# The odd layer's five engine queues, ordered by a planner in the kernel instead of by the framework's scheduler

## The chip, the cores and the metric

The kernel runs on one core of a Trainium2 chip. The metric is the device time of one launch in microseconds (us), less being better. The core has five instruction queues that run side by side, each strictly in order: TensorE (PE, matmuls), VectorE (DVE), ScalarE (ACT), GpSimd (POOL), and SyncE (SP), which here issues the DMA transfers. An instruction at the head of its queue that waits for another engine or a transfer holds up all that stand behind it in that queue.

## The reference

A trunk of two layers over 1024 tokens of width 1024, all float32, and a final RMSNorm. The even layer (dilated attention and HGRN2, with one output projection) isn't touched. The odd layer is a gated DeltaNet with 8 key heads of 128, each with two value heads of 128:

```python
def gated_delta_rule_chunked(q, k, v, g, beta):
    # S_t = exp(g_t)(I - b_t k_t k_t^T) S_{t-1} + b_t k_t v_t^T ; o_t = S_t^T q_t
    ...
    def step(state, inp):
        u_n, w_n, a_n, qd_n, kt_n, gl_n = inp
        v_new = u_n - jnp.einsum('bhcd,bhdv->bhcv', w_n, state)
        o = jnp.einsum('bhcd,bhdv->bhcv', qd_n, state) + jnp.einsum('bhij,bhjv->bhiv', a_n, v_new)
        new_state = state * gl_n[..., None, None] + jnp.einsum('bhcd,bhcv->bhdv', kt_n, v_new)
        return new_state, o

def odd_mixer(hn, w_in, conv_w, dt_bias, a_log, norm_w, w_out):
    qkv, z, b_logit, a_logit = _split(hn @ w_in, ODD_SIZES)
    qkv = jax.nn.silu(causal_depthwise_conv(qkv, conv_w))
    q, k, v = _split(qkv, (C_KEY_WIDTH, C_KEY_WIDTH, C_VAL_WIDTH))
    ...  # l2-normalized q and k, beta = sigmoid(b_logit), g from a_logit
    o = gated_delta_rule_chunked(q, k, v, g, beta)
    o = rms_norm(o, norm_w) * jax.nn.silu(z)
    return o.reshape(bsz, s, C_VAL_WIDTH) @ w_out

for layer in range(DEPTH):
    hn = rms_norm(h, norm_w[layer])
    h = h + (odd_mixer(hn, ...) if layer % 2 else even_mixer(hn, ...))
return rms_norm(h, final_norm_w)
```

## The kernel before

**Matmuls.** A float32 product is made of three matmuls over high and low parts (`hi·hi`, `lo·hi`, `hi·lo`; L151 to L153). `cut` loads a weight slice by SP (`raww`, L115), makes the high part on ACT (`w_hi`, L116) and the low part on DVE (`w_lo`, L117). `norm_T` (L207 to L227) norms a tile of 128 tokens, transposes it on PE (`nt`) and writes `hn_hi` on ACT and `hn_lo` on DVE.

**The odd layer** (from L817) starts with `gates` (L828 to L887: PE's `abp`, its copy `ab` on ACT, then exponentials, decays and their running sums). Then for each key head: `proj` makes the projections `pk`, `pv`, `pq` and `oz` (the gate `z`), `conv` the short convolution on ACT and DVE (L892 to L908), `turn_k`, `turn_q` and `turn_v` transpose and normalize. `invert` (L1045 to L1146) inverts the triangular matrix of all chunks of a head: `kk` on PE (L1063), `L` on DVE (L1069) with its copy on ACT (L1118), 62 small steps `tm` and `Tp` in turn on DVE (L1084, L1086), a transposition `Un` (L1090), and the small matmuls `qp`, `up`, `q` and `u` (L1107 to L1138).

`recur` (L1149 to L1225) then goes through the head's 8 chunks of 128 tokens, a chain from engine to engine. For each chunk: `ks` (PE, L1182) to `r` (DVE, L1185); `qs` (PE, L1188) to `oq` (ACT, L1191); `vp` (PE, L1197) to `vt` (DVE, L1200) and to its copy `vn` (ACT, L1202); `kv` (PE, L1206) to the new state `S` (DVE, L1210), which the next chunk's `ks` needs; `op` (PE, L1217) from `vn` and `A`; the result `bv` (DVE, L1220). Beside it run `qk` and `A` for the next chunk (L1168, L1170), with decays `gca` that are loaded by DMA, masked on POOL (L1156) and raised on ACT (L1158). When a head is done, `normed` scales it on POOL (`bv`, L1005), and `gated` transposes it (`ot`, PE), scales it (`oy`, ACT L1013), multiplies it by the gate (POOL L1014) and stores it.

**Order.** The text of the program mixes these: `mix` and `blend` take a step of the filling work whenever the main work has run up a debt, as in

```python
mix(recur(hh), fill, 2.8)
```

where `fill` holds the next head's `invert` and `proj` and the output of a head before. In the odd layer the order on each queue is then set by the framework's own scheduler, with the program's order as priority. In parts of the even layer the program sets the order on PE itself. Tiles are taken from tags with a few buffers each (in PSUM: `pj`, `a` and `b` two each, `c` and `d` one each); a new tile waits until the one whose place it takes has been read.

In the row names below, `vp4_3` is head 4, chunk 3; a last number is the buffer's.

Of the kernel before, what the change touches and what calls it, by code (L numbers as in the profile page):

```python
# [79 lines left out]


@with_exitstack
def trunk_kernel(ctx: ExitStack, tc: tile.TileContext, x, ew, ewo, ow, owab, owo, nw, fnw, lbl, hnw,
                 cw, dtb, alog, onw, cst, out):
    nc = tc.nc
    dve, act, pe, pool = nc.vector, nc.scalar, nc.tensor, nc.gpsimd

# [14 lines left out]
    def load_row(dst, row):  # L102
        nc.sync.dma_start(dst, bass.AP(tensor=row.tensor, offset=row.offset, ap=[[0, P], [1, row.shape[-1]]]))

# [8 lines left out]
    def cut(src, hi, lo, name):  # L113
        raw = wp.tile([P, 512], F32, name=f"raw{name}", tag="raw", bufs=2)
        nc.sync.dma_start(raw, src)  # L115
        act.copy(hi, raw)  # L116
        dve.tensor_tensor(lo, raw, hi.bitcast(F32), op=ALU.subtract)  # L117
# [9 lines left out]
    def load_unit():  # L127
        i, (src, n) = next(queue, (0, (None, 0)))
        if src is owab:
            raw = wp.tile([P, KC * 32], F32, name="wab", tag="lo", bufs=NW)  # L130
            nc.sync.dma_start(raw, src)
            return raw
        parts = []
        drain(unit_steps(parts, i, src, n))
        return parts
# [187 lines left out]
    def even_layer(es):  # L323
# [30 lines left out]
        lt = sm.tile([P, nl, 8], F32, name="lt", bufs=1)  # L354
        nc.sync.dma_start(lt, lbl.rearrange("l p h -> p l h"))
        nc.sync.dma_start(xs[0], x[0:128, :])
        dve.tensor_copy(lm, lt[:, 0, :])
# [19 lines left out]
        for t in range(NT):  # L377
            if t:
                xs.append(big(("osb", "x", "tot", "sg")[t % 4], f"x{t}"))
                nc.sync.dma_start(xs[t], x[t * 128:(t + 1) * 128, :])  # L380
            else:
                load_row(nwb, nw[0])
                nc.sync.dma_start(ident, cst[:, C_ID:C_ID + 128])
# [4 lines left out]
        nc.sync.dma_start(masks, cst[:, C_LV:C_LV + 80].rearrange("p (l c) -> p l c", l=5))  # L388
        id32 = sm.tile([P, 32], F32, name="id32", bufs=1)
        nc.sync.dma_start(id32, cst[:, C_ID32:C_ID32 + 32])  # L390
        hw = sm.tile([P, 1], F32, name="hw", bufs=1)
        nc.sync.dma_start(hw, hnw)
        def values(b, name, copies):
# [56 lines left out]
        def hgrn_chain(b):  # L450
# [104 lines left out]
            for h in range(2):  # L555
                tp = bank("d", [P, 512], f"bt{b}_{h}")
                for c in range(4):
# [3 lines left out]
                                   op=ALU.mult)  # L561
            nc.sync.dma_start(ymix[D + b * 128:D + (b + 1) * 128, :], y)

# [118 lines left out]
        def weigh(p):  # L682

            rd = RD[p]
            rp = bank("a", [2 * NT, 128], f"rp{p}")
            pe.matmul(rp, rd.rearrange("p e t -> p (e t)"), PM, start=True, stop=True)
            rs = sm.tile([2 * NT, 128], F32, name=f"rs_{p}", tag="rs_")
            act.copy(rs, rp)
            rdd = dp.tile([2 * NT, 128], F32, name=f"rdd{p}")
            nc.sync.dma_start(rdd, rs)  # L690
            y = Y[p] = big("y", f"ay{p}")
            for e in range(2):
                nc.sync.dma_start(y[64 * e:64 * e + 64], bass.AP(tensor=rdd.tensor, offset=rdd.offset + e * T, ap=[[0, 64], [1, T]]))
# [75 lines left out]
        def after(t):  # L769
            if t == 0:  # L770
                hn_tiles()
                nwb1.append(big("nwb", "nwb1"))
                load_row(nwb1[0], nw[1])
            nc.sync.dma_start(h1[t * 128:(t + 1) * 128, :], h2[t])
            norm_T(h2[t], t, sm, nwb1[0], big("xn", f"xn1_{t}"))
# [8 lines left out]
        G = at.tile([P, WG], F32, name="G")  # L784
        nc.sync.dma_start(G, cst[:, C_G:C_G + WG])
        PM = at.tile([P, 128], F32, name="PM")
        nc.sync.dma_start(PM, cst[:, C_PM:C_PM + 128])
        PB = at.tile([P, 2, NT * WG + 192], F32, name="PB")
# [27 lines left out]

    def odd_layer(es):  # L817
        sp = es.enter_context(tc.tile_pool(name="od", bufs=1))
        gt = {n: sp.tile([P, NT, 16], F32, name=f"g_{n}") for n in ("beta", "gc", "ngc", "eg", "nbeg", "etl", "egl")}
        MA = sp.tile([P, 128], F32, name="MA")  # L820
        nc.sync.dma_start(MA, cst[:, C_MA:C_MA + 128])
        cws = sp.tile([P, 32, 4], F32, name="cws")
        nc.sync.dma_start(cws, cw)
        ow_ = sp.tile([P, 1], F32, name="onws")
        nc.sync.dma_start(ow_, onw)
        dve.tensor_scalar(ow_, ow_, 0.5, None, op0=ALU.mult)

        def gates():  # L828

            cs = sp.tile([P, 4, 128], F32, name="gcs_", tag="T64")  # L830
            tri, ones, dt, ea = cs[:, 0, :], cs[:, 1, :], cs[:, 2, 0:16], cs[:, 2, 16:32]
            nc.sync.dma_start(tri, cst[:, C_TRI:C_TRI + 128])
            id32 = cs[:, 2, 32:64]
            nc.sync.dma_start(id32, cst[:, C_ID32:C_ID32 + 32])
            dve.memset(ones, 1.0)
# [50 lines left out]
            act.copy(cs[:, 3, :], tq)  # L886
            nc.sync.dma_start(gcd, cs[:, 3, :])  # L887
            yield 0.0, 0.1
# [119 lines left out]
        def gated(hh, e, h, g):  # L1008
# [5 lines left out]
            pool.tensor_tensor(y, y, g, op=ALU.mult)  # L1014
            nc.sync.dma_start(ymix[(2 * hh + e) * 128:(2 * hh + e + 1) * 128, h * 512:h * 512 + 512], y)

# [21 lines left out]
        def decays(hh, c, w):  # L1038
            g = sp.tile([P, 2, 128], F32, name=f"gc{w}{hh}_{c}", tag=f"gc{w}", bufs=2)
            nc.sync.dma_start(g, bass.AP(tensor=gcd.tensor, offset=gcd.offset + (c * 16 + 2 * hh) * 128,  # L1040
                                         ap=[[0, P], [128, 2], [1, 128]]))
            return g

        def invert(hh):
# [186 lines left out]
        def hres(t, g=None):  # L1231
            r = hr[t // 4][:, t % 4, :]
            return (r, r) if g is not None else r

        def y_parts(g):
# [5 lines left out]
            def then():  # L1241
                for t in range(NT):
                    nc.sync.dma_start(hres(t), h1[t * 128:(t + 1) * 128, :])

            return yh, yl, 0, then

        def after(t):
# [3 lines left out]
            for n in range(0, D, m):  # L1251
                dve.scalar_tensor_tensor(o[:, n:n + m], hres(t)[:, n:n + m], rs, nwf[:, n:n + m], op0=ALU.mult, op1=ALU.mult)  # L1252
                nc.sync.dma_start(out[t * 128:(t + 1) * 128, n:n + m], o[:, n:n + m])

# [94 lines left out]
```

## Time and profile before

| | us |
|---|---|
| median of 3 runs (lowest, highest) | 2273.03 (2270.43, 2273.27) |
| profiled execution, its time | 2270.35 |
| profiled execution, its span | 2268.6 |
| mean granted PE clock | 0.992 |

The profiled execution was thus 2.7 us faster than the median, and its span leaves out 1.75 us of launch. The odd layer's first matmul starts at 1193.1 us of the span, and the layer lasts until the end. Engine times are busy times; a matmul's record is longer than the distance to the next one's start, since they overlap. Rows of the trace have their start, their length, engine, line, operation, tile written and tiles read, shapes, how many alike were joined, and in brackets the idle time of the engine ahead and who ended it.

### The profile page before, as it was taken

Reading aid. Unit: us, or ns where it says so; the run is one execution under the profiler, and the core shown is the slowest. Engines: PE = TensorE matmul, PEld = TensorE weight load, DVE = VectorE, ACT = ScalarE, POOL = GpSimd, SP = SyncE. Lnnn points to the kernel's source line nnn. Section 1 sums busy time; section 2 is a strip of 40 time slices with the busy share of each in tenths; the row PEclk is TensorE's granted clock in tenths of the full one; section 3 lists DMA queues with packets and bytes.
Section 4 is the critical chain, followed back from the end, with each engine's and each line's share of the span. In section 5 each row is a group of like instructions: output and inputs, shape, how many; then the busy total and the mean of one; then the engine's idle time right before and its main releaser. Section 6 shows DMA issues by size and latency. Waiting matters only on the chain. (4 is left out here: it accounts for less than half of the span.)

```text
span 2268.6 us, 52553 instructions
## 1 busy us (share of the span) xinstructions
PE 2162.0 (95%) x21781; PEld 1760.6 (78%) x21781; DVE 1409.7 (62%) x3236; ACT 950.0 (42%) x2551; POOL 239.5 (11%) x252
## 2 busy tenths in 40 slices
PE   7999999999999999989999988989898999899998
PEld 6888888898877878767886776767777777678787
DVE  6353535453444344457776986968878787755767
ACT  5233333333232232222237664655555555544223
POOL 0010101010000000000000013121212121210000
PEclk9999999999999999989999999999999999999999
DMA  4111111114342334353233222121212122124233
GB/s 146 38 48 48 43 49 47 48 34 126 91 128 71 109 91 122 97 162 108 93 116 104 61 55 67 51 78 41 77 51 76 49 71 65 58 64 153 85 112 112
DMA packets 100079, 184.15 MB, mean 81 GB/s; under 512 B 12672, under 2 KB 30208, under 8 KB 99840
## 3 DMA queue, kind: packets, MB, share of 16 engines
q1 hardware_dynamic: 99840, 180.79, 25.9%
q8 instruction: 171, 2.80, 0.5%
q14 instruction: 68, 0.56, 0.1%
HBM read 151.25 MB, written 29.49 MB: 80 GB/s over the span
## 5 line engine op out<-in xcount | busy, mean ns | idle before, releaser
L117 DVE TENSOR_TENSOR w_lo<-raww,w_hi 128x512 fp32r<-128x512 f32 x292 | 210.2, 722 | 199.5 <-ACT w_hi L116 196.8
L116 ACT CAST w_hi<-raww 128x512 fp32r<-128x512 f32 x292 | 181.1, 620 | 298.0 <-DMA raww<-in_ewo_dram 51.0
L647 ACT ACTIVATE P<-P,nm 128x256 f32<-128x256 f32 (+7 forms) x128 | 71.4, 559 | 133.9 <-DVE nm L645 133.9
L151 PE MATMUL op<-w_hi,yplo 128*128 128x512 f32 x288 | 113.7, 395 | 3.3 <-DVE hr L296 1.7
L153 PE MATMUL op<-w_hi,yplo 128*128 128x512 f32 x288 | 112.2, 390 | 0.0
L152 PE MATMUL op<-w_lo,yplo 128*128 128x512 f32 x288 | 112.2, 390 | 0.0
L151 PE MATMUL oz<-hn_hi,w_hi 128*128 128x512 f32 x256 | 109.9, 429 | 0.0
L151 PE MATMUL pv<-hn_hi,w_hi 128*128 128x512 f32 x256 | 106.7, 417 | 0.5 <-ACT uv L899 0.5
L296 DVE TENSOR_TENSOR hr<-hr,op 128x512 f32<-128x512 f32 x128 | 85.9, 684 | 34.2 <-PE op L153 33.6
L153 PE MATMUL pv<-hn_hi,w_lo 128*128 128x512 f32 x256 | 104.1, 407 | 0.0
L152 PE MATMUL oz<-hn_lo,w_hi 128*128 128x512 f32 x256 | 103.0, 402 | 0.0
L153 PE MATMUL oz<-hn_hi,w_lo 128*128 128x512 f32 x256 | 102.5, 400 | 0.0
L152 PE MATMUL pv<-hn_lo,w_hi 128*128 128x512 f32 x256 | 102.2, 399 | 0.0
L653 DVE STREAM_TRANSPOSE PB<-P 128x256 f32<-128x256 f32 (+3 forms) x64 | 54.6, 853 | 72.8 <-ACT P L647 72.8
L1156 POOL TENSOR_TENSOR gca<-gca,MA 128x256 f32<-128x256 f32 x64 | 50.6, 791 | 453.8 <-DMA gca<-gcd 252.8
L296 DVE TENSOR_TENSOR hres<-hres,op 128x512 f32<-128x512 f32 x96 | 64.7, 682 | 31.8 <-PE op L153 29.4
L642 DVE CUSTOM_DVE_ANT_0 P<-S,G 128x256 f32<-128x256 f32 (+7 forms) x128 | 58.2, 492 | 36.8 <-PE S L638 35.2
L904 DVE SCALAR_TENSOR_TENSOR vT<-uv,cws,vT 128x512 f32<-128x512 f32 x96 | 74.3, 774 | 4.7 <-ACT vT L902 3.8
L1084 DVE TENSOR_TENSOR tm<-Lp,Tp 128x126 f32<-128x126 f32 (+22 forms) x248 | 74.9, 302 | 3.7
L1158 ACT ACTIVATE gca<-gca,g_ngc 128x128 f32<-128x128 f32 x128 | 45.8, 401 | 69.3 <-POOL gca L1156 69.1
L151 PE MATMUL avp<-w_hi,hn_hi 128*128 128x256 f32 x256 | 74.5, 291 | 0.0
L151 PE MATMUL op<-w_hi,yphi 128*128 128x512 f32 x160 | 65.9, 412 | 8.5 <-ACT yphi L116 4.6
(367 smaller groups left out, 6292.1 us busy)
## 6 DMA issues: line engine op xcount, KB each, us to landing
raww<-in_ew_dram SPq DMA_DIRECT2D x128, 256.0 KB, 3.0
raww<-in_ow_dram SPq DMA_DIRECT2D x100, 256.0 KB, 3.0
V<-vd SPq DMA_DIRECT2D x64, 256.0 KB, 5.3
rawy<-ymix SPq DMA_DIRECT2D x64, 256.0 KB, 2.7
raww<-in_ewo_dram SPq DMA_DIRECT2D x32, 256.0 KB, 3.0
gcl<-gcd SPq DMA_DIRECT2D x64, 128.0 KB, 3.0
gca<-gcd SPq DMA_DIRECT2D x64, 128.0 KB, 3.0
ymix<-oy SPq DMA_DIRECT2D x32, 256.0 KB, 2.0
```

Of the source, the lines that this page charges most:

```text
L116: act.copy(hi, raw)
L117: dve.tensor_tensor(lo, raw, hi.bitcast(F32), op=ALU.subtract)
L151: pe.matmul(ps, lh, rh, start=start, stop=False)
L152: pe.matmul(ps, lh, rl, start=False, stop=False)
L153: pe.matmul(ps, ll, rh, start=False, stop=stop)
L296: dve.tensor_tensor(dst[:, n], src[:, n], ps, op=ALU.add)
L642: dve.tensor_tensor_reduce(Pm[:, e, w0:], S[e][:, w0:WG], G[:, w0:], 1.0, -3e38, op0=ALU.add, op1=ALU.max, accum_out=mx[:, e:e + 1])
L647: act.activation(Pm[:, e, w0:], Pm[:, e, w0:], AF.Exp, bias=nmx[:, e:e + 1], scale=0.125, accum_out=den[:, i, e:e + 1])
L653: dve.transpose(PB[:, :, i * WG + w0:(i + 1) * WG], Pm[:, :, w0:])
L904: dve.scalar_tensor_tensor(a[0][:, s], ub[:, i + s.start:i + s.stop], cws[:, tile_no, i:i + 1], a[0][:, s], op0=ALU.mult, op1=ALU.add)
L1084: dve.tensor_tensor(tm[:, :31 - k, :n], Lp[:, k, k + 1:, None].to_broadcast([P, 31 - k, n]), Tp[:, k:k + 1, :n].to_broadcast([P, 31 - k, n ...
L1156: pool.tensor_tensor(DA, DA, MA[:, None, :].to_broadcast([P, 2, 128]), op=ALU.add)
```

## The change

Every engine handle is wrapped in a `Lane`. While `plan.ops` is a list, which is so from the first line of `odd_layer` to its end, a call is recorded and not issued. At the end `Plan.run` builds a graph: which recorded instruction reads or overwrites what another wrote (`edges`, by the bytes touched), and for each tag, which tile must be done before its place is used again. It then goes through time from 0 with five free engines: the engine that can start something soonest takes, of its instructions that are ready by then, the one that stands first in the program. Lengths come from `times`, a small table by engine, operation and size; a result that goes to another engine counts as there after a further 500 ns (to PE) or 300 ns (to the others). `Plan.give` issues everything in the order of the planned starts, with all five queues' order fixed to that. The even layer's instructions pass through as before and are no part of the plan. No instruction is added or left out on PE, DVE, ACT or POOL. The odd layer's instructions all have one line in the changed kernel (L270); tiles keep their names.

```diff
+class Plan:
+    SEM = {"PE": 500, "DVE": 300, "ACT": 300, "POOL": 300, "SP": 300}
...
+    def times(self, op, last):
+        if key == "SP":
+            return 420, 3200
+        if key == "PE":
+            if name == "transpose":
+                return 109, 280
...
+                held = n / 2.4 * (1 if r32 else 4) + (14 if r32 else 8)
...
+            return held, held + 190
+        if key == "DVE":
...
+            elif n < 20:
+                t = 85
+            elif n >= 512:
+                t = 100 + 1.15 * n
+            else:
+                t = 70 + 1.08 * n
+            return t, t + 80
+        if key == "ACT":
+            t = 210 + 0.75 * n if n > 128 else 300
...
+            return t, t + 95
...
+        t = 780 if n <= 256 or a[0].ap[0][1] == 32 else 1330
+        return t, t + 40
...
+    def run(self):
+        pred, gates = self.dag = self.edges()
...
+                if k is None or k == key and k not in ("PE", "SP"):
+                    t = done
+                else:
+                    t = 0.0 if k == key == "PE" else done + self.SEM[k]
...
+        while done_n < n:
+            best = None
+            for k in keys:
+                if ready[k]:
+                    s = max(free[k], min(at[i] for i in ready[k]))
+                    if best is None or s < best[0]:
+                        best = s, k
...
+            s, k = best
+            i = min(i for i in ready[k] if at[i] <= s)
+            ready[k].remove(i)
+            held, got = self.times(ops[i], last)
+            starts[i] = s
+            free[k] = s + held
+            release(i, s + got, k)
+            done_n += 1
+
+    def give(self):
+        order = sorted(range(len(self.ops)), key=lambda i: (self.starts[i], i))
+        ops, self.ops = self.ops, None
+        for i in order:
+            ops[i]["f"](*ops[i]["a"], **ops[i]["kw"])
...
+    plan = Plan()
+    dve, act, pe, pool, sync = (plan.lane(*z) for z in (("DVE", nc.vector), ("ACT", nc.scalar), ("PE", nc.tensor),
+                                                       ("POOL", nc.gpsimd), ("SP", nc.sync)))
...
-        nc.sync.dma_start(raw, src)
+        sync.dma_start(raw, src)
...
     def odd_layer(es):
+        plan.ops = []
...
         drain(blend(way_out7(), out_last(range(3, 8), ["pj", "b"])))
+        plan.run()
+        with tc.manual_schedule(engines={getattr(mybir.EngineType, n) for n in ("PE", "DVE", "Activation", "Pool", "SP")}):
+            plan.give()
```

(The DMAs elsewhere change from `nc.sync` to `sync` in the same way.)

**ACT in a middle head.** The rows around head 4's chunk 3, where `vn4_3` is the copy that `op4_3` needs and `gca4_5` the decay of a chunk two further on. Before:

```order
L1225 ACTIVATE oj4_2_0_20440,oss4_19863<-bv4_19691 128x128
L1225 ACTIVATE oj4_2_1_20442,oss4_19863<-bv4_19691 128x128
L1191 ACTIVATE oq4_3_20495<-qs4_3_20493,g_eg_14220 128x128 x2
L1158 ACTIVATE gca4_5_20552<-gca4_5_20552,g_ngc_14219 128x128 x2
L1202 COPY vn4_3_20520<-vp4_3_20515 128x256
L1225 ACTIVATE oj4_3_0_20562,oss4_19863<-bv4_19691 128x128
```

After:

```order
L270 ACTIVATE oj4_2_0_15573,oss4_15448<-bv4_15421 128x128
L270 ACTIVATE oj4_2_1_15574,oss4_15448<-bv4_15421 128x128
L270 ACTIVATE oq4_3_15593<-qs4_3_15592,g_eg_14220 128x128 x2
L270 COPY vn4_3_15597<-vp4_3_15595 128x256
L270 ACTIVATE gca4_5_15603<-gca4_5_15603,g_ngc_14219 128x128 x2
L270 COPY uk6_15588<-pk6_0_15589 128x512
L270 ACTIVATE kT6_15624<-uk6_15588,cws_14225 128x512
```

The two `oq` stand first in both; `vn4_3` now stands ahead of `gca4_5` and not behind it.

**ACT at the seam between the layers.** `w39` is the even layer's last weight, `w41` the odd layer's first (its `pk0` on PE reads it), `xn1`, `sd` and `hn_hi` are steps of the last norm. Before:

```order
L116 CAST w39_hi2_13750<-raww39_2_13752 128x512
L116 CAST w39_hi3_13756<-raww39_3_13758 128x512
L116 CAST w41_hi0_14238<-raww41_0_14240 128x512
L116 CAST w41_hi1_14244<-raww41_1_14246 128x512
L116 CAST w41_hi2_14250<-raww41_2_14252 128x512
L207 ACTIVATE xn1_0_13915,ss0_13916<-hres0_12079 128x1024
L212 ACT_TABLE_LOAD
L212 ACTIVATE sd0_13918<-ss0_13916,epsc_70 128x1
L207 ACTIVATE xn1_1_13954,ss1_13955<-hres1_12080 128x1024
```

After, at the end of that norm:

```order
L284 CAST hn_hi0_13908<-nt6_0_14157 128x4x128
L284 ACTIVATE sd7_14191<-ss7_14189,epsc_70 128x1
L284 CAST hn_hi1_13909<-nt6_1_14164 128x4x128
L284 CAST hn_hi0_13908<-nt7_0_14196 128x4x128
L284 CAST hn_hi1_13909<-nt7_1_14203 128x4x128
L270 COPY ab_14240<-abp0_14241 128x512
L270 ACT_TABLE_LOAD
L270 ACTIVATE gcs__14227<-gcs__14227 128x16
L270 CAST w41_hi0_14228<-raww41_0_14230 128x512
L270 CAST w41_hi1_14231<-raww41_1_14233 128x512
```

Before, three `w41` casts stood ahead of the norm's first tile; now they stand behind its last, behind the copy `ab`, a table load and an exponential of `gates`. On PE, `pk0` moves in the same way behind the norm's last transpositions.

**PE in head 0.** The rows from chunk 3's `op` to chunk 4's `vp`. Before:

```order
L1217 MATMUL op0_3_15912<-vn0_3_15883,A0_3_15800 128x128 x2
L1168 MATMUL qk0_4_15920<-q0_15141,kT0_14333 128x128
L1182 MATMUL ks0_4_15935<-S0_3_15909,kT0_14333 128x256
L151 MATMUL oz0_0_0_16296<-hn_hi0_13908,w46_hi0_15818 128x512
L1188 MATMUL qs0_4_15940<-S0_3_15909,q0_15141 128x256
L152 MATMUL oz0_0_0_16296<-hn_lo0_13910,w46_hi0_15818 128x512
L153 MATMUL oz0_0_0_16296<-hn_hi0_13908,w46_lo0_15819 128x512
L151 MATMUL oz0_0_0_16296<-hn_hi0_13908,w46_hi0_15818 128x512
L152 MATMUL oz0_0_0_16296<-hn_lo0_13910,w46_hi0_15818 128x512
L153 MATMUL oz0_0_0_16296<-hn_hi0_13908,w46_lo0_15819 128x512
L151 MATMUL oz0_0_0_16296<-hn_hi1_13909,w46_hi1_15824 128x512
L1197 MATMUL vp0_4_15986<-r0_4_15937,L0_14534 128x128 x2
```

After, from chunk 3's `vp`:

```order
L270 MATMUL vp0_3_14558<-r0_3_14554,L0_14294 128x128 x2
L270 MATMUL op0_3_14565<-vn0_3_14560,A0_3_14535 128x128
L270 MATMUL kv0_3_14563<-vt0_3_14559,kn0_14292 128x256
L270 MATMUL op0_3_14565<-vn0_3_14560,A0_3_14535 128x128
L270 MATMUL qk0_4_14567<-q0_14392,kT0_14256 128x128
L270 MATMUL ks0_4_14571<-S0_3_14564,kT0_14256 128x256
L270 MATMUL qs0_4_14573<-S0_3_14564,q0_14392 128x256
L270 MATMUL vp0_4_14580<-r0_4_14572,L0_14294 128x128 x2
```

Before, the gate's projection `oz` filled the places between the chain's steps; now chunks 3 to 7 of head 0 stand with nothing between, and the `oz` rows have moved ahead of chunk 3 or behind the head.

More of the change, by code (lines that the diff above doesn't have):

```diff
@@ L82, in trunk_kernel, with __init__, __getattr__, call @@
+class Lane:
+    def __init__(self, plan, key, engine):
+        self.plan, self.key, self.engine = plan, key, engine
+    def __getattr__(self, name):
+        f = getattr(self.engine, name)
+        def call(*a, **kw):
+            if self.plan.ops is None:
+                return f(*a, **kw)
+            self.plan.add(self.key, f, name, a, kw)
+        return call
 @with_exitstack
@@ L102, in load_row @@
     def load_row(dst, row):
-        nc.sync.dma_start(dst, bass.AP(tensor=row.tensor, offset=row.offset, ap=[[0, P], [1, row.shape[-1]]]))
+        sync.dma_start(dst, bass.AP(tensor=row.tensor, offset=row.offset, ap=[[0, P], [1, row.shape[-1]]]))
     queue = [(ew[i], 4) for i in (*range(16, 32), *range(16))] + [(ewo[g], 4) for g in range(8)] + [(owab, 0)]
@@ L130, in load_unit @@
             raw = wp.tile([P, KC * 32], F32, name="wab", tag="lo", bufs=NW)
-            nc.sync.dma_start(raw, src)
+            sync.dma_start(raw, src)
             return raw
@@ L354, in even_layer @@
         lt = sm.tile([P, nl, 8], F32, name="lt", bufs=1)
-        nc.sync.dma_start(lt, lbl.rearrange("l p h -> p l h"))
-        nc.sync.dma_start(xs[0], x[0:128, :])
+        sync.dma_start(lt, lbl.rearrange("l p h -> p l h"))
+        sync.dma_start(xs[0], x[0:128, :])
         dve.tensor_copy(lm, lt[:, 0, :])
@@ L379, in even_layer @@
                 xs.append(big(("osb", "x", "tot", "sg")[t % 4], f"x{t}"))
[L380 removed]
+                sync.dma_start(xs[t], x[t * 128:(t + 1) * 128, :])
             else:
                 load_row(nwb, nw[0])
[L383 removed]
+                sync.dma_start(ident, cst[:, C_ID:C_ID + 128])
             norm_T(xs[t], t, sm, nwb, big("y", f"xn{t}"))
         masks = sm.tile([P, 5, 16], F32, name="lvm", bufs=1)
[L388 removed]
+        sync.dma_start(masks, cst[:, C_LV:C_LV + 80].rearrange("p (l c) -> p l c", l=5))
         id32 = sm.tile([P, 32], F32, name="id32", bufs=1)
[L390 removed]
+        sync.dma_start(id32, cst[:, C_ID32:C_ID32 + 32])
         hw = sm.tile([P, 1], F32, name="hw", bufs=1)
[L392 removed]
+        sync.dma_start(hw, hnw)
         def values(b, name, copies):
@@ L784, in even_layer @@
         G = at.tile([P, WG], F32, name="G")
-        nc.sync.dma_start(G, cst[:, C_G:C_G + WG])
+        sync.dma_start(G, cst[:, C_G:C_G + WG])
         PM = at.tile([P, 128], F32, name="PM")
-        nc.sync.dma_start(PM, cst[:, C_PM:C_PM + 128])
+        sync.dma_start(PM, cst[:, C_PM:C_PM + 128])
         PB = at.tile([P, 2, NT * WG + 192], F32, name="PB")
@@ L820, in odd_layer @@
         MA = sp.tile([P, 128], F32, name="MA")
-        nc.sync.dma_start(MA, cst[:, C_MA:C_MA + 128])
+        sync.dma_start(MA, cst[:, C_MA:C_MA + 128])
         cws = sp.tile([P, 32, 4], F32, name="cws")
-        nc.sync.dma_start(cws, cw)
+        sync.dma_start(cws, cw)
         ow_ = sp.tile([P, 1], F32, name="onws")
-        nc.sync.dma_start(ow_, onw)
+        sync.dma_start(ow_, onw)
         dve.tensor_scalar(ow_, ow_, 0.5, None, op0=ALU.mult)
@@ L886, in gates @@
             act.copy(cs[:, 3, :], tq)
-            nc.sync.dma_start(gcd, cs[:, 3, :])
+            sync.dma_start(gcd, cs[:, 3, :])
             yield 0.0, 0.1
@@ L1252, in after @@
                 dve.scalar_tensor_tensor(o[:, n:n + m], hres(t)[:, n:n + m], rs, nwf[:, n:n + m], op0=ALU.mult, op1=ALU.mult)
-                nc.sync.dma_start(out[t * 128:(t + 1) * 128, n:n + m], o[:, n:n + m])
+                sync.dma_start(out[t * 128:(t + 1) * 128, n:n + m], o[:, n:n + m])
         def out_last(groups, tags):
```

149 lines of the change are left out of this document (133 added, 16 removed).

## The prediction

> **What bounds the kernel now.** I read the page first, then a table of engine times by stage, then PE's waits in the long stage, then single instructions in order of time. The page says that PE is the bound.
>
> ```profile
> span 2268.6 us, 52553 instructions
> PE 2162.0 (95%) x21781; PEld 1760.6 (78%) x21781; DVE 1409.7 (62%) x3236; ACT 950.0 (42%) x2551; POOL 239.5 (11%) x252
> ```
>
> The next view splits the span by stage; its columns are busy time and count on PE, PEld, DVE, ACT and POOL, then the granted clock, DMA share and GB/s. The first stretch ends where the odd layer's first matmul starts; the second is its beginning (gates, head 0's projection, the first invert), the third is recurrence head 0, the fourth heads 1 to 6, the fifth head 7 with the output projection.
>
> ```profile
> 0.00:1193.00 1193.00, 1165.20 (x15320) 959.34 (x15320) 592.17 (x1208) 396.59 (x975) 71.22 (x68) 0.99 0.29 87
> 1193.00:1319.30 126.30, 118.86 (x800) 91.54 (x800) 104.06 (x261) 82.33 (x211) 7.72 (x11) 1.00 0.25 72
> 1319.30:1401.10 81.80, 71.06 (x541) 55.73 (x540) 63.61 (x178) 43.40 (x128) 19.86 (x24) 0.94 0.22 62
> 1401.10:2022.00 620.90, 571.35 (x4042) 460.55 (x4041) 491.53 (x1312) 349.24 (x1051) 120.72 (x132) 0.99 0.21 62
> 2022.00:2262.00 240.00, 235.52 (x1083) 193.41 (x1081) 155.22 (x273) 77.49 (x186) 20.01 (x20) 1.00 0.32 112
> ```
>
> So PE stands idle for 126.30 − 118.86 = 7.4 us in the beginning, 81.80 − 71.06 = 10.7 in head 0, 620.90 − 571.35 = 49.6 in heads 1 to 6 and 4.5 after that. The change leaves every matmul in, so only idle time and what hangs on it can move. Heads 1 to 6 hold the pool. PE's waits there (who waits, for whom; total us, times, longest):
>
> ```profile
> PE ks L1182 <- DVE S L1210: 9.7, 7, 1.8
> PE op L1217 <- ACT vn L1202: 7.4, 9, 1.6
> PE vp L1197 <- ACT oq L1191: 6.3, 9, 1.6
> PE kk L1063 <- DVE L L1069: 5.7, 4, 1.5
> PE q L1130 <- ACT L L1118: 4.6, 5, 2.5
> PE vp L1197 <- DVE r L1185: 3.9, 4, 1.0
> PE up L1114 <- DVE Q L1109: 3.1, 4, 1.2
> ```
>
> These seven lines are 40.7 of the 49.6 us: short waits of about 1 us, where DVE or ACT is late, though neither is full (DVE 491.53 of 620.90, ACT 349.24). A record also overstates busy PE: consecutive 512-wide matmuls start 0.23 us apart but last 0.39.
>
> ```profile
> 1734.23 0.39 PE L153 MATMUL pk<-hn_hi,w_lo 128*128 128x512 f32 x1
> 1734.46 0.40 PE L151 MATMUL pk<-hn_hi,w_hi 128*128 128x512 f32 x1
> ```
>
> So each stall costs about 0.39 − 0.23 = 0.16 us more than its idle time: the seven lines' 42 waits and the smaller ones, about 60, add 10. **Pool: 49.6 + 10 = about 59 us.**
>
> **Part 1, the order in heads 1 to 6.** Why are DVE and ACT late? An example from head 4 (two rows of ACT, then PE):
>
> ```profile
> 1741.77 0.69 ACT L1158 ACTIVATE gca<-gca,g_ngc 128x128 f32<-128x128 f32 x2 [2.22 <-POOL gca L1156]
> ...
> 1742.37 0.35 ACT L1202 COPY vn<-vp 128x256 f32<-128x256 f32 x1
> ...
> 1742.77 0.71 PE L1217 MATMUL op<-vn,A 128*128 128x128 f32 x4 [0.92 <-ACT vn L1202]
> ```
>
> ACT had `vn` queued behind `gca`, which waited 2.22 us for POOL and is wanted only a chunk later; PE then sat 0.92 us. The changed order has `vn` first here. It is a wait made by order alone, and the planner, which places an instruction only when its inputs are there by its own clock, takes such waits out. Its clock is roughly that of the trace: 594 ns for a 512-wide ACT copy (a row below has 0.62 us), 402 for the 256-wide `vn` (0.35 above). Its hops are long: from DVE's end to PE's start it counts 80 + 500 ns, and the trace has 1736.84 + 0.33 to 1737.32, or 0.15 us:
>
> ```profile
> 1735.51 1.26 POOL L1014 TENSOR_TENSOR oy<-oy,g 128x512 f32<-128x512 f32 x1 [3.79 <-ACT oy L1013]
> 1735.76 1.16 DVE L1084 TENSOR_TENSOR tm<-Lp,Tp 128x126 f32<-128x126 f32 x1
> ...
> 1736.84 0.33 DVE L1210 SCALAR_TENSOR_TENSOR S<-S,g_egl,kv 128x128 f32<-128x128 f32 x1
> ...
> 1737.32 0.67 PE L1182 MATMUL ks<-S,kT 128*128 128x256 f32 x2 [1.77 <-DVE S L1210]
> ```
>
> So a consumer is placed some 0.4 us later than it could run, which leaves slack for small errors. Against that stands what the plan cannot know: DVE is slowed while POOL runs.
>
> ```profile
> 1374.50 0.24 DVE L1084 TENSOR_TENSOR tm<-Lp,Tp 128x78 f32<-128x78 f32 x1
> ...
> 1375.56 0.95 DVE L1084 TENSOR_TENSOR tm<-Lp,Tp 128x70 f32<-128x70 f32 x1
> ...
> 1375.38 4.03 POOL L1005 TENSOR_TENSOR bv<-bv,ors 128x512 f32<-128x512 f32 x4
> ```
>
> A 0.24 us step takes 0.95 beside POOL's 4.03/4 = 1.0 us instructions, 0.7 more. Heads 1 to 6 hold 132 POOL instructions, 22 a head; where one meets an instruction that PE waits for soon, the 0.4 us of slack doesn't cover it. [...]
>
> How much of the pool goes? At least nothing (all 49.6 us are then new waits of the same size), at most all of it. Of the seven lines, `op` and `vp` behind ACT, `q` behind ACT and `up` behind DVE (7.4 + 6.3 + 4.6 + 3.1 = 21.4 of 40.7, 53%) wait for an engine that is 56% to 79% busy, so for order. `ks` behind `S` (9.7) is partly POOL's doing: in the rows above the second `S` stood behind a `tm` that took 1.16 us beside POOL, and `ks` waited 1.77 for it. In the new order each hop of the chain has 1.6 us or more of other matmuls in it in heads 2 to 6 (counted in the order, 0.23 us each). I take 60%, near the 53% plus half of the rest that isn't POOL's, bounds 30% and 90%: **−36 us (−18 to −53).**
>
> **Part 2, the seam between the layers.** The plan starts from an empty machine: it sees nothing of the even layer, and the odd layer's instructions all follow the even layer's on each ordered queue. Before, weights `w41` were loaded and cut ahead of the last norm (ACT, rows shown above), and PE began `pk` at 1198.71. Now the first `w41` cast stands behind the last `hn_hi`, the copy `ab`, a table load and an exp on ACT. Those rows of before:
>
> ```profile
> 1198.71 0.50 PE L151 MATMUL pk<-hn_hi,w_hi 128*128 128x512 f32 x1
> ...
> 1204.00 1.07 ACT L226 CAST hn_hi<-nt 128x512 fp32r<-128x512 f32 x2 [0.49 <-PE nt L224]
> ...
> 1204.96 0.61 ACT L850 COPY ab<-abp 128x512 f32<-128x512 f32 x1
> ...
> 1206.75 0.62 ACT L116 CAST w_hi<-raww 128x512 fp32r<-128x512 f32 x1
> ...
> 1208.27 1.28 ACT L838 ACT_TABLE_LOAD   x1
> ```
>
> 1204.00 + 1.07 + 0.61 + 1.28 + 0.2 (exp, taken like a small ACT step) + 0.62 gives `pk` at about 1207.8, 9.1 us later. In those 9.1 us PE had 32 matmuls of `pk`, by 0.23 us 7.4; the rest were `nt` and waits, which stay. The last `hn_hi` comes earlier by up to four casts that are gone from ahead of it on ACT, 4 × 0.62 = 2.5 us, of which I take half. SP's loads of `w41` also stand behind the h1 writes and the odd layer's small loads; I let them land by then. At most all 9.1 is lost. **+6 us (3 to 9).**
>
> **Part 3, head 0.** The planner takes fill matmuls as early as they are ready. By the order, 40 projection matmuls (512 wide, 9 us) move ahead of the first `vp`; between head 0's first `vp` and head 1's they fall from 154 to 78 (17 us fewer), and 36 more stand in head 1. From chunk 3 of head 0 to head 1's first `vp` PE holds only the recurrence and the next invert, since the next gate's bank is free only once head 0 is normalized. Without fill the end is set by DVE and by the hops:
>
> ```profile
> 1319.30:1382.90 63.60, 53.67 (x275) 42.10 (x273) 55.02 (x163) 36.34 (x115) 11.39 (x14) 0.97 0.22 59
> 1382.90:1401.10 18.20, 17.39 (x266) 13.63 (x267) 8.60 (x16) 7.06 (x13) 8.47 (x10) 0.83 0.22 71
> ...
> 1382.94 0.71 DVE L1090 STREAM_TRANSPOSE Un<-Tn 128x512 f32<-128x512 f32 x1
> ```
>
> DVE is busy for 55.02 of the 63.6 us up to `Un`. Summed by their lengths in this trace, its instructions from head 0's first `vt` to `Un` are 65.4 us by the order of before (the records overlap a little) and 58.6 by the new one, so the stretch needs 63.6 × 58.6/65.4 = 57 us. The 18.2 us from there to the next head held 36 fills (8 us): 14 to 18 now, 71 to 75 in all. Break-even is today's 81.8 − 17.4 = 64.4. So **+8 us (3 to 14)**, between 71 − 64.4 = 6.6 and 75 − 64.4 = 10.6; less if DVE's part shrinks with the stretch, more if the hops add to DVE's work instead of lying beside it.
>
> The bare stretch has a second risk. The clock fell to half right there, after two windows with PE half busy:
>
> ```profile
> 1372.20:1375.60 3.40, 1.64 (x8) 1.02 (x6) 3.37 (x20) 0.14 (x1) 0.90 (x2) 1.00 0.14 39
> 1375.60:1379.00 3.40, 1.31 (x6) 0.60 (x6) 3.30 (x4) 1.24 (x3) 3.40 (x4) 1.00 0.00 0
> 1379.00:1382.40 3.40, 2.58 (x10) 1.85 (x10) 3.16 (x8) 1.18 (x2) 1.64 (x2) 0.50 0.22 80
> ```
>
> [...] Worked out from rows, it is a rival below.
>
> **Costed at nothing.** Head 7, output projection and tail: the order there is nearly the same, PE has 4.5 us idle in 240. The same number of table loads and of changes between kinds of matmul remains. SP: weight loads move by some rows within the queue; `raww` loads have had whole chunks of time ahead of their casts, at 0.21 of the DMA engines.
>
> **Sum.** −36 + 6 + 8 = −22 us. The profiled execution took 2270.35 us (span 2268.6), 2.7 under the median of 2273.03, so 2248 for such an execution and 2273 − 22 = 2251, rounded to 2250, against the median.
>
> **Rivals.** Changes under 0.2% (4.5 us) can't be told from none.
>
> 1. *Slower: the fixed order brings its own waits.* [...] If as much comes as goes, 6 + 8 remain: 2287. It decides once less than 14/59 = 24% of the pool goes, less the 4.5 that can't be told: 16%. For it: DVE is 79% busy there. Against: before has the same POOL work under an order that knew as little of it. 0.15.
> 2. *No change*: 16% to 31% of the pool goes and the seam and head 0 eat it: 2273. 0.10.
> 3. *The clock halves in head 0's bare stretch.* A bare chunk has `vp`, `op`, `kv`, `ks`, `qs` and `qk`: by rows like 0.71 (`op`) and 0.67 (`ks`), less an overlap of 0.16 or more each, 2.4 to 2.9 us. Four such chunks at half speed take 10 to 12 more: 2262. For it: the windows above, with PE busy for 1.31 and 1.64 of 3.4. Against: DVE paces that stretch anyway. 0.12.
> 4. *Nearly all stalls go*: 53 + 14 gives −53 + 14 = −39, 2234; with a better seam 2231. For it: hops with 1.6 us of fill. Against: POOL. 0.17.
> 5. *It doesn't do what it says* (the orders come out alike): the order of rows shows otherwise in heads, seam and head 0.
>
> **Chances.** The forecast (45 to 75% of the pool) 0.46, its own range 2240 to 2259. Faster: 0.46 + 0.12 + 0.17 = 0.75; same 0.10; slower 0.15. The range goes from the fourth rival's 2231 to just above no change, 2276, and leaves the first out.
>
> **What would show it.** In the trace after: PE's idle time from head 1's first `vp` to head 7's falls from 49.6 to 15 to 30 us and `op` behind `vn` leaves the list of waits, while `ks` behind `S` stays in part (step 1); PE idle or waiting for the `w41` cast until about 1207 (step 2); chunks 3 to 7 of head 0 with a gap on PE at each hop, and its clock (step 3). I am wrong if heads 1 to 6 still take 103 us each, which would make the order not their limit, or if the seam costs over 10 us.

## The result

The changed kernel took 2234.76 us (median of 4 runs, 2230.55 to 2237.47) against 2272.88 for the kernel before, a ratio of 0.9833 with a 95% interval of 0.9816 to 0.985: **38 us faster**. 2250 was forecast, with a range of 2231 to 2276. In a later comparison of the same two the ratio was 0.9824 (0.981 to 0.9837).

The page after:

```profile
span 2233.6 us, 52459 instructions
PE 2162.9 (97%) x21781; PEld 1780.9 (80%) x21781; DVE 1393.5 (62%) x3236; ACT 947.2 (42%) x2551; POOL 239.2 (11%) x252
```

The same matmuls took 35 us less. The table by stage has its borders where the odd layer starts and at the first `vp` of heads 0, 1 and 7 (columns as before):

```profile
0.00:1193.79 1193.79, 1164.37 (x15320) 959.20 (x15320) 590.14 (x1205) 395.01 (x973) 71.00 (x68) 0.99 0.28 86
1193.79:1340.30 146.51, 132.86 (x820) 102.71 (x820) 108.69 (x269) 84.59 (x217) 7.80 (x10) 0.94 0.23 70
1340.30:1412.50 72.20, 59.93 (x458) 48.22 (x457) 55.49 (x168) 35.88 (x114) 15.65 (x20) 0.77 0.19 48
1412.50:1982.30 569.80, 567.77 (x4099) 474.17 (x4098) 476.61 (x1312) 352.00 (x1061) 120.41 (x133) 0.99 0.24 68
1982.30:2227.00 244.70, 237.93 (x1091) 196.55 (x1089) 159.27 (x280) 78.24 (x185) 24.31 (x22) 0.99 0.32 110
```

PE's idle time in heads 1 to 6 is 569.80 − 567.77 = **2.0 us, where it was 49.6**. DVE is busy for 477 us there where it was 492, ACT for 352 where it was 349. All that is left of the list of PE's waits there:

```profile
PE kv L270 <- DVE vt L270: 0.9, 1, 0.9
PE kk L270 <- DVE uk L270: 0.4, 2, 0.2
PE ks L270 <- DVE tm L270: 0.4, 1, 0.4
PE kk L270 <- DVE uv L270: 0.2, 1, 0.2
PE q L270 <- issue: 0.2, 1, 0.2
```

Neither `op` behind `vn` nor `ks` behind `S` is in it. The next table takes out what was only moved: the projections' 512-wide matmuls, which the new order spreads otherwise over the stretches, at 0.23 us each. Times are distances between the starts of the first matmuls named, from their rows, in us.

| stretch | before | after | moved matmuls | net change | forecast |
|---|---|---|---|---|---|
| `abp` to head 0's `vp` | 124.5 | 146.5 | +40, +9.1 | +13 | +6 |
| head 0's `vp` to head 1's | 81.8 | 72.2 | −76, −17.4 | +8 | +8 |
| heads 1 to 6 | 622.0 | 569.7 | +36, +8.2 | −60.5 | −36 |
| head 7 to the end | 247.2 | 251.3 | 0 | +4 | 0 |

With 0.7 us in the even layer the net changes add up to −35, the difference of the spans (2268.6 to 2233.6).

**The seam.** The rows around the layer's first weights, from SP, ACT and PE:

```profile
1204.27 1.63 PE L284 MATMUL nt<-ident,xn 128*128 128x128 f32 x8 [2.68 <-DVE xn L284]
1205.97 0.33 SPq L270 DMA_DIRECT2D MA<-in_cst_dram  x1
...
1209.19 0.91 SPq L270 DMA_DIRECT2D raww<-in_ow_dram  x2
1209.66 1.89 PE L270 MATMUL abt<-gcs__14227,ab 128*128 128x32 f32 x8 [3.76 <-DMA gcs__14227<-in_cst_dram]
...
1212.41 0.62 ACT L270 CAST w_hi<-raww 128x512 fp32r<-128x512 f32 x1 [0.83 <-DMA raww<-in_ow_dram]
...
1213.08 0.79 PE L270 MATMUL pk<-hn_hi,w_hi 128*128 128x512 f32 x1 [1.54 <-ACT w_hi L270]
```

The load of the mask `MA` goes out just after PE's last `nt` of the old layer; I read that as waiting for its place in memory, which no run tested. The weight's load stands behind it on SP, with the other small ones, and goes out at 1209.19, not at 1191 to 1199 as before. `pk` begins at 1213.1 and not at the 1207.8 that I had worked out (0.7 of the 5.3 us come from the even layer), and its next matmuls start 0.43 us apart (1213.67, 1214.10) and not 0.23; the granted clock was 0.50 from 1213 to 1218 us, and over the whole stretch it is 0.94 on average.

**Head 7.** One wait of 4.5 us, of PE for `oq`. First the DMA view of that place (queue, count, KB each, median us to landing), then rows of ACT and PE:

```profile
hr<-h SPq DMA_DIRECT2D x8, 512.0 KB, 7.2
rawy<-ymix SPq DMA_DIRECT2D x3, 256.0 KB, 8.9
...
2043.89 0.62 ACT L270 CAST yplo<-rawy 128x512 fp32r<-128x512 f32 x1 [6.83 <-DMA rawy<-ymix]
...
2045.23 0.61 ACT L270 ACTIVATE oq<-qs,g_eg 128x128 f32<-128x128 f32 x2
...
2045.90 1.22 PE L270 MATMUL vp<-r,L 128*128 128x128 f32 x4 [4.49 <-ACT oq L270]
```

Eight loads of 512 KB went out together; `rawy` behind them landed after 8.9 us, where the plan counts 3.2 us for any DMA. Its casts were queued on ACT ahead of `oq`.

### The profile page after: what moved, and what is told of

The parts are those of the page before. It is cut to its first block, busy times and chain, and to the rows that moved or that the text cites. A ratio compares the mean times of both kernels' runs of the same rounds, so it can differ in the third digit from the quotient of the medians.

```text
span 2233.6 us, 52459 instructions
## 1 busy us (share of the span) xinstructions
PE 2162.9 (97%) x21781; PEld 1780.9 (80%) x21781; DVE 1393.5 (62%) x3236; ACT 947.2 (42%) x2551; POOL 239.2 (11%) x252
## 3 DMA queue, kind: packets, MB, share of 16 engines
q1 hardware_dynamic: 99840, 180.79, 26.5%
## 5 line engine op out<-in xcount | busy, mean ns | idle before, releaser
L270 PE MATMUL op<-w_hi,yplo 128*128 128x512 f32 x448 | 140.4, 392 | 0.7 <-DVE hr L270 0.6
L270 ACT CAST w_hi<-raww 128x512 fp32r<-128x512 f32 x132 | 81.8, 621 | 89.8 <-DMA raww<-in_owo_dram 42.8
L270 DVE TENSOR_TENSOR hr<-hr,op 128x512 f32<-128x512 f32 x128 | 87.4, 685 | 48.7 <-PE op L270 46.2
L284 PE MATMUL op<-w_hi,yphi 128*128 128x512 f32 x320 | 105.9, 405 | 7.9 <-DVE hres L284 4.8
L270 DVE TENSOR_TENSOR w_lo<-raww,w_hi 128x512 fp32r<-128x512 f32 x132 | 96.3, 732 | 20.5 <-ACT w_hi L270 17.5
L270 PE MATMUL pv<-hn_hi,w_hi 128*128 128x512 f32 x256 | 107.4, 419 | 0.0
L270 PE MATMUL oz<-hn_hi,w_hi 128*128 128x512 f32 x256 | 107.3, 419 | 0.0
L270 PE MATMUL pv<-hn_hi,w_lo 128*128 128x512 f32 x256 | 103.6, 405 | 0.0
L270 PE MATMUL pv<-hn_lo,w_hi 128*128 128x512 f32 x256 | 102.4, 400 | 0.0
L270 PE MATMUL oz<-hn_hi,w_lo 128*128 128x512 f32 x256 | 102.2, 399 | 0.0
L270 PE MATMUL oz<-hn_lo,w_hi 128*128 128x512 f32 x256 | 101.9, 398 | 0.0
L270 PEld LDWEIGHTS op<-w_hi,yplo 128*128 128x128 f32 x448 | 84.1, 188 | 18.9 <-DVE hr L270 1.5
L270 POOL TENSOR_TENSOR gca<-gca,MA 128x256 f32<-128x256 f32 x64 | 54.6, 854 | 366.0 <-DMA gca<-gcd 196.3
L270 PE MATMUL op<-w_lo,yplo 128*128 128x512 f32 x224 | 86.9, 389 | 0.0
L284 PEld LDWEIGHTS op<-w_hi,yphi 128*128 128x128 f32 x320 | 62.0, 194 | 23.8 <-DVE hres L284 5.6
```

The source lines that it names most:

```text
L270: ops[i]["f"](*ops[i]["a"], **ops[i]["kw"])
L284: return f(*a, **kw)
```

## The experiments

Times are medians; each ratio is to the kernel before, run on the same chip. Stretches are read from one profiled execution each, and two executions of the changed kernel itself (the second is that of the comparison further down) gave 72.2 and 70.2 us for head 0, 569.7 and 571.3 for heads 1 to 6: a difference of 2 us in a stretch shows little.

**Which queues need the plan?** Two kernels fix the plan's order on some engines and leave the others to the framework's scheduler, with the planned order as priority.

```diff
-... for n in ("PE", "DVE", "Activation", "Pool", "SP")}
+... for n in ("PE",)}                                    # PE alone
+... for n in ("DVE", "Activation", "Pool", "SP")}        # all but PE
```

> The changed kernel with the plan's order fixed on PE alone; on DVE, ACT, POOL and SP the framework's scheduler sets the order, with the planned order as its priority. Theory 1, the order of DVE and ACT is what went wrong before (vn behind gca): without it fixed, waits of PE for DVE and ACT come back, 15 to 40 us, and the run takes 2250 to 2275. Rival, the order of PE against the others is what matters: 2231 to 2241. If PE's fixed order meets engines that are ordered for something else, it can be slower than before, over 2280.

> The changed kernel with the plan's order fixed on DVE, ACT, POOL and SP, and not on PE, where the framework's scheduler sets the order with the planned order as its priority. Theory 1, what was wrong before is the order on DVE and ACT: with it fixed, PE's order by priority is nearly the plan's, and the run stays within 10 us of the changed kernel. Rival, all queues must be of one plan, as the run with PE alone fixed suggests (2320): PE's other order meets fixed queues, over 2260.

PE alone: **2320.25 us, 1.0213 (1.019 to 1.0236)**, slower than before the change. All but PE: 2237.58, 0.9833 (0.982 to 0.9847), no different from the change itself. In the first, PE's order is the plan's but for a few rows; its idle time in heads 1 to 6 is 653.10 − 597.35 = 55.8 us:

```profile
1416.30:2069.40 653.10, 597.35 (x4097) 484.89 (x4098) 499.32 (x1316) 353.97 (x1059) 126.19 (x133) 0.96 0.21 60
...
PE kv L270 <- DVE vt L270: 15.0, 13, 3.1
PE ks L270 <- DVE S L270: 8.7, 8, 2.0
```

So, with PE in the plan's order in both, the gain hangs on the order of the other queues: PE's order alone gains nothing. What PE's order is worth is not shown, since PE, left to priorities, came out nearly as planned: by the tile names in the trace of the second, all but some 50 of the odd layer's 6461 matmul rows follow the plan's sequence. Nor do these two runs tell DVE's order from ACT's.

**Is DVE's slowing beside POOL what would have stayed?** The kernel before, with the two longest kinds of POOL's instructions cut to a few elements, so that it leaves out most of those products:

```diff
-pool.tensor_tensor(bv[:, t:t + 2], bv[:, t:t + 2], rs[...].to_broadcast([P, 2, 2, 128]),
+pool.tensor_tensor(bv[:, t:t + 2, :, 0:4], bv[:, t:t + 2, :, 0:4], rs[...].to_broadcast([P, 2, 2, 4]),
-            pool.tensor_tensor(y, y, g, op=ALU.mult)
+            pool.tensor_tensor(y[:, 0:8], y[:, 0:8], g[:, 0:8], op=ALU.mult)
```

> The kernel before, with POOL's normalization (L1005) and its product with the gate (L1014) cut to 4 and 8 of the elements of a row; the rest of those products is left out. gca's mask stays. [...]

The prediction took 60% of the pool to go; the 40% left, some 24 of 59 us, it put down in part to DVE slowed beside POOL. With less of POOL's work, then, the run should be shorter. It took 2268.33 us, 0.999 (0.9979 to 1.0001). Heads 1 to 6 are no shorter with POOL at 78 us in place of 121:

```profile
1395.40:2020.10 624.70, 577.81 (x4058) 470.11 (x4058) 481.74 (x1312) 346.73 (x1053) 78.16 (x133) 0.98 0.21 61
...
PE vp L1197 <- ACT oq L1191: 9.3, 7, 3.3
PE op L1217 <- ACT vn L1202: 8.3, 9, 1.4
PE vp L1197 <- DVE Tp L1086: 8.0, 3, 3.0
...
PE ks L1182 <- DVE S L1210: 0.7, 1, 0.7
```

`ks` behind `S` did fall from 9.7 to 0.7 us, but `vp` behind `Tp`, which wasn't in the list, is 8.0. Two reserves. The framework's scheduler orders this smaller program somewhat differently, so it doesn't show what each wait is worth. And only a part of the slowing is gone: counting DVE instructions at least 0.1 us above the median of their kind, all of them beside a POOL instruction, heads 1 to 6 hold 32 with 14 us of excess, where the kernel before holds 53 with 23 by this count. So taking out some 40% of the slowing gained nothing under such orders; what taking out all of it would do is not shown.

**Is it the plan's long hops?**

```diff
-    SEM = {"PE": 500, "DVE": 300, "ACT": 300, "POOL": 300, "SP": 300}
+    SEM = {"PE": 70, "DVE": 70, "ACT": 70, "POOL": 70, "SP": 70}           # short
+    SEM = {"PE": 1000, "DVE": 800, "ACT": 800, "POOL": 800, "SP": 800}     # long
```

> The changed kernel with the planner's hops cut to 70 ns on every engine (500 and 300 before), about what the trace shows between engines (0.15 us with the 80 ns already in a length). Theory 1, slack: the long hops keep consumers some 0.4 us later than they could run, and this absorbs what the plan does not know, the slowing of DVE beside POOL above all; then stalls come back in heads 1 to 6, 15 to 40 us of the 59 us pool, and the run takes 2250 to 2275. Rival, order alone: any list schedule with roughly right lengths does it; PE's idle time in heads 1 to 6 stays under 8 us and the run within 6 us of 2235.

> The changed kernel with longer hops in the planner: 1000 ns to PE and 800 to the others, in place of 500 and 300. Theory, slack: PE's idle time in heads 1 to 6 was already 2 us, so there is nothing left to gain there; where the chain stands bare (head 0, the start), instructions of other work are put ahead of the chain's more often: the run within 6 us of 2235, rather slower. Rival, more slack is better everywhere: faster by over 5 us. If the planner then runs out of filling work, PE idles by order: slower by 10 to 40 us.

Short: 2254.98 us, 0.993 (0.9915 to 0.9945), about 23 slower than the change by the two ratios; the loss is in heads 1 to 6, where PE is idle for 590.10 − 575.59 = 14.5 us, while head 0 takes 67.9 us in place of 72.2 (with 15 of the 512-wide matmuls, 3.4 us, moved ahead of it):

```profile
1411.30:2001.40 590.10, 575.59 (x4103) 471.98 (x4103) 487.23 (x1318) 355.52 (x1060) 118.31 (x134) 0.99 0.23 66
...
PE ks L270 <- DVE S L270: 4.9, 7, 1.1
PE kk L270 <- DVE L L270: 3.9, 9, 0.4
```

Five of the waits of `ks`, four for `S` and one for `Tp`, 5.1 us together, have the pattern that the prediction showed, a `tm` slowed beside POOL just ahead of what `ks` needs:

```profile
1736.88 1.27 POOL L270 TENSOR_TENSOR oy<-oy,g 128x512 f32<-128x512 f32 x1 [3.23 <-ACT gca L270]
...
1737.09 1.19 DVE L270 TENSOR_TENSOR tm<-Lp,Tp 128x115 f32<-128x115 f32 x1
...
1738.69 0.67 PE L270 MATMUL ks<-S,kT 128*128 128x256 f32 x2 [1.11 <-DVE S L270]
```

The next `tm`, of nearly that size and with POOL idle, takes 0.26 us (at 1738.99). So with short hops POOL's slowing does reach PE, for about a third of the idle time; the other waits for DVE have no slowed instruction, by the count above, just ahead of them.

Long: 2322.59, 1.0242 (1.0226 to 1.0257), which neither 'within 6 us' nor 'faster' had; only the last clause had a loss, and a smaller one. Its order puts all the fill up to head 1 ahead of head 0's first `vp` (504 matmuls; the change 426), and heads 1 to 6 hold 55 more 512-wide matmuls than in the change (13 us), with PE idle for 35.5 us and a clock of 0.93, where the change had 0.99:

```profile
1427.90:2079.00 651.10, 615.59 (x4147) 511.62 (x4146) 485.37 (x1320) 354.72 (x1067) 120.29 (x140) 0.93 0.21 62
```

So a hop planned longer than it is (80 + 500 ns planned, 0.15 us in the prediction's rows) works as slack, up to a point: of the three settings, 70 ns is too little, 300 and 500 are enough, 800 and 1000 far too much.

**Do the measured lengths matter?** One length for all instructions of DVE, ACT and POOL:

```diff
             held, got = self.times(ops[i], last)
+            if k in ("DVE", "ACT", "POOL"):
+                held, got = 400, 480
```

> The changed kernel with one length for all DVE, ACT and POOL instructions in the plan: 400 ns (480 to the result) in place of the table's 85 to 1950. Theory, measured lengths matter: DVE's plan is then wrong by up to 1.5 us an instruction, the order misplaces the chain's instructions, waits come back and the run takes 2255 to 2300. Rival: with the dependences and long hops, the order hardly depends on lengths: within 8 us of 2235.

2287.6 us, 1.0091 (1.0073 to 1.011): some 59 us slower than the table by the ratios, and slower than the framework's own order. Heads 1 to 6 take 605.5 us, with PE idle for 26.5. The hops were those of the change, so slack alone doesn't do it: with this one wrong length more than the whole gain is lost.

**The seam**, with `w41` asked for before recording begins:

```diff
     def odd_layer(es):
+        w_ab = unit()
         plan.ops = []
...
-            w = unit().rearrange("p (k j) -> p k j", k=KC)
+            w = w_ab.rearrange("p (k j) -> p k j", k=KC)
```

> The changed kernel with one edit: the odd layer's first weights (w41) are asked for ahead of the first recorded instruction, so they are not part of the plan. Theory 1, the seam: SP issued w41's load only after the h1 writes, the mask MA, which waits until 1206 us for its place, and six more small loads, so pk began at 1213.1 instead of 1198.7; with the load ahead of these, pk begins at about 1199 again, the time from the layer's first matmul to head 0's first vp falls from 146.5 us to about 133, and the run from 2235 to about 2222 (-10 to -15). Rival: DVE's and ACT's chain of gates and the first invert sets that time, not PE; then pk begins earlier but vp does not, and the run gains under 4 us.

`pk` begins at 1199.7, but head 0's first `vp` comes 137.9 us after `abp`: 8.6 less than 146.5, not the 13 that `pk` gained. 2227.94 us, 0.9808 (0.9787 to 0.9828). The interval overlaps that of the change; the stretch in the trace is clear.

**Head 0**, with a second gate buffer on top of that:

```diff
-... tag="g")
+... tag="g", bufs=2)
-... tag="oy", bufs=2)
+... tag="oy", bufs=1)
```

> The kernel of the run with w41 asked for ahead of the plan, with two buffers for the gate tiles g in place of one, and one for oy in place of two to make room. By the order, 24 more projection matmuls (5.5 us) then stand between head 0's chunks 3 and 5. Theory, fill: head 0's bare stretch idles PE because the next gate has no place; first vp of head 0 to that of head 1 holds 5.5 us more work in about the same 72 us, and the run gains 4 to 8 us on that kernel. Rival, DVE's chain sets head 0's length and the fill moves the chain back as much: gain under 2 us. With one oy buffer, way_out can stall instead: then slower by a few us.

2228.09 us, 0.9819 (0.9805 to 0.9834): no gain on the run before. Head 0 took 73.9 us with 24 more matmuls against 71.6, and head 1 95.9 against 93.9 though it held 9 fewer. So head 0 did take in 5.5 us of matmuls for 2.3 us more, and the layer as a whole gained nothing by it; whether the lost `oy` buffer took the gain back in head 1 was not told apart.

**DMAs planned by their bytes:**

```diff
         if key == "SP":
-            return 420, 3200
+            held = max(420, 1.28 * n)
+            return held, held + 2780
```

> The changed kernel with one edit in the planner's table: a DMA holds SP for the time of its bytes at 400 GB/s (1.31 us for 512 KB, 0.66 for 256 KB) and lands 2.78 us later, in place of 0.42 and 3.2 us for all. Theory: head 7 lost 4 us since eight 512 KB loads went out at 2029 us, the rawy loads behind them landed after 8.9 us and not 3.2, and ACT had their casts queued ahead of oq, for which PE waited 4.5 us; with the bytes counted, oq stands ahead of the cast that waits, vp7_0 to the end falls from 248.4 to about 243 us, and the run by 4 to 7 us. Rival: another wait takes its place in the output projection, since the transfers are as long as they are; the run stays within 2 us.

The edit's 400 GB/s is near the 391 that the trace of the change shows from 2031 to 2040 us, while the eight loads ran. The run took 2225.01 us, 0.9814 (0.9799 to 0.9829), an interval that overlaps that of the change. In the trace PE's wait of 4.5 us for `oq` is gone; head 7 to the end of the last record fell from 248.4 to 244.7, and heads 2 to 6 by 3 more. That 3.7 was to be 5.

**Both, and the hops between:**

> The changed kernel as it is, for a comparison with the two that follow on the same chip. All theories: 0.983 of the kernel before, about 2230 to 2236 us.

> The changed kernel with both edits that gained by themselves: w41 asked for ahead of the plan, and DMAs planned by their bytes. If the two costs lie in different places (the seam, and head 7 with the output projection), the gains add: first vp after the seam 8 us earlier, vp7_0 to the end 4 us shorter, together 8 to 12 us under the changed kernel of this call. Rival: the new order of the whole layer that either edit brings changes heads 1 to 6 by as much; then within 4 us of the better of the two.

> The run before this one with hops of 350 ns to PE and 200 to the others, in place of 500 and 300. By the runs so far, 70 ns costs 20 us and 1000/800 costs 88. Theory 1, slack has a flat optimum: heads 2 to 6 within 5 us of 475, head 0 some us shorter as with 70 ns (67.9 in place of 72.2): 0 to 5 us faster than that run. Rival, every bit of slack counts: heads 1 to 6 lose 5 to 12 us, and the run is slower by as much.

On one chip: the change 2235.35 (0.9824), **both edits 2211.26, 0.9725 (0.9712 to 0.9739), the fastest kernel of this study**, and both with hops of 350 and 200 ns 2216.47, 0.9741 (0.9727 to 0.9754). Both edits give 24 us, more than the 8 to 12 expected. 15.3 lie at the start (131.5 us to the first `vp`, where the seam edit alone had 137.9), 4.6 in head 7 to the end, 4.6 in heads 1 to 6:

```profile
1193.50:1330.00 136.50, 131.63 (x870) 103.45 (x861) 111.96 (x280) 85.37 (x217) 7.44 (x11) 1.00 0.23 70
```

The clock at the start is 1.00, where the change had 0.94; the seam edit alone still has waits of 4.2 (`pv` for `uv`) and 2.0 us there. Why the two together gain more than each alone was not told apart. The shorter hops lose 6.7 us in heads 2 to 6 (480.8 in place of 474.1) and win 3.4 at the start, where 15 matmuls (3.4 us) were only moved on into head 0. In total they are 5 us slower, with intervals that overlap: slack counts little between these two.

## Why the prediction was right, and where it was not

The direction, the mechanism and the range held: the pool of about 59 us in heads 1 to 6 was about right (60.5 went), and the waits made by order vanished. What came is the fourth rival, nearly all stalls gone. That its 2234 was met is luck in part: more went in heads 1 to 6 than its 53, and more was lost elsewhere (25) than its 14. The forecast itself was 15 us too slow (its own range, 2240 to 2259, should read 2243 to 2260 by the shares given, on which nothing hangs): three terms of the sum were mis-sized, 24.5 us one way and 11 the other, and 3 us are the difference between medians and profiled executions (38 against 35).

- **Part 1, the order: −36 was −60.5.** The step that failed is "60%", with the bound at 90%. I held back the part that I put down to POOL slowing DVE: the sign named was 15 to 30 us of idle time with `ks` behind `S` in it, and 2.0 us without it came. In the changed kernel DVE is still slowed beside POOL (in heads 1 to 6, by the count above, 34 instructions with 17 us more than the median of their kind, 53 with 23 before; by what means, no run shows), and PE doesn't wait. Hops too long by 0.4 us, which I had found and thought too small a cover for 0.7, do cover it here: cut to 70 ns, 14.5 us of idle time came back, 5.1 of them right behind a slowed `tm`. That the fill matmuls between the steps help in it is argued, not shown.
- **Part 2, the seam: +6 was +13.** By the sign that I had named (over 10 us) I was wrong here. I traced the ACT queue and let SP's loads "land by then". They didn't: the load stood behind `MA`, and PE began 5.3 us later than worked out, at a clock of 0.50 for its first 5 us. The seam edit took 8.6 us of this stretch back, with planned DMA bytes 15.
- **Part 3, head 0: +8 was +8**, but not for the reason given alone. Up to `Un` it took the 57.0 us that were worked out, though DVE's instructions there sum to about 54 us in this trace and not to 58.6, so the agreement is luck in part. The clock halved there, as in the third rival, after windows with PE busy for 1.91 and 2.11 of 3.4 us:

```profile
1372.20:1375.60 3.40, 1.91 (x9) 1.24 (x9) 3.18 (x14) 1.57 (x7) 0.00 (x0) 1.00 0.17 39
1375.60:1379.00 3.40, 2.11 (x10) 1.66 (x11) 3.27 (x12) 0.69 (x2) 0.84 (x1) 0.95 0.00 0
1379.00:1382.40 3.40, 2.46 (x7) 1.35 (x6) 2.73 (x11) 1.40 (x7) 0.66 (x1) 0.50 0.14 39
```

  It stayed at 0.50 to the end of the head. The rows of PE in these windows show no wait of over 1.00 us (that of `ks` for `S`, at 1378.43):

```profile
1372.27 0.67 PE L270 MATMUL ks<-S,kT 128*128 128x256 f32 x2 [0.82 <-DVE tm L270]
1372.78 0.59 PE L270 MATMUL qs<-S,q 128*128 128x256 f32 x2
1374.33 0.71 PE L270 MATMUL vp<-r,L 128*128 128x128 f32 x4 [0.96 <-ACT oq L270]
...
1381.01 1.22 PE L270 MATMUL vp<-r,L 128*128 128x128 f32 x4 [0.78 <-ACT oq L270]
```

  What makes the clock fall is not shown; the price was far under the 10 to 12 us of the rival. The three bare chunks from 1374.33 on (`vp` at 1374.33, 1381.01, 1388.24, 1395.27) took 20.9 us, 16.6 of them at half clock. In the second execution of this kernel the clock stayed up for longer, and the same three took 19.0 (`vp` at 1373.69, 1380.13, 1386.72, 1392.69), with 3.4 us at half. Its head 0 as a whole, with 17.5 us at half clock in place of 33.9:

```profile
1339.70:1409.90 70.20, 54.84 (x459) 44.33 (x458) 55.17 (x168) 36.01 (x114) 16.18 (x20) 0.88 0.23 50
```

  So 16 us less at half clock went with 2.0 us less time; at that rate, an estimate from two executions, the clock is some 4 of the 8 us. The rest was not told apart, and more fill there did not shorten the layer.
- **Costed at nothing: head 7, +4.** I let SP's transfers be covered and compared only how alike the orders were. The 4.5 us wait is the first rival's kind, a wait that the fixed order brings, in a place I hadn't priced.
- **The first rival** (new waits eat the gain) did not come with this table of hops and lengths, but it is what flat lengths, long hops, or PE alone under the plan give: 2288, 2323, 2320.

## What to carry to other kernels

The in-order queues of the kernel before stalled each other by what stood ahead, though DVE was busy for only 79% and ACT for 56% of heads 1 to 6: a list schedule with measured lengths and hops planned 0.3 to 0.5 us took out 48 of 50 us of PE's idle time in six heads. Planning PE's queue alone lost 2%; fixing the other four, with PE left to priorities from the plan, did as well as fixing all five. Such a plan depends on its lengths, and what it doesn't see it gets wrong: look first at its seam with other work, above all at the DMA queue, and at transfers whose size it ignores. When a moved step is costed, walk every queue that it stands in to what its head waits for.

## What the runs showed that I had not expected

Planned hops that are too long cost more than hops that are too short: against 500 and 300 ns, 70 ns costs about 23 us and 1000 and 800 about 93. DVE's slowing beside POOL (a `tm` of 70 columns took 0.95 us beside it in the kernel before, one of 78, begun 0.2 us ahead of POOL, 0.24) reaches PE or not by the slack in the order: five slowed `tm` held `ks` up for 5.1 us under hops of 70 ns, and under 300 and 500 all of PE's waits in heads 1 to 6 are 2.0 us. And PE's clock halved, from 1.00 to 0.50, in a chain of small matmuls with PE busy for 56% and 62% of two windows of 3.4 us and no wait over 1.00 us; no sharp limit is shown, since in the second execution of the same kernel the clock stayed full through four windows of 3.4 us with PE busy for 1.85 to 2.11.
